# A decoder layer in float32r: new start addresses for the weight slots, and the transposed activations laid out four row tiles side by side

## The chip, the cores and the metric

The kernel runs on one core of a Trainium2 chip. The metric is the device time of one execution in microseconds (us). Before the change the median of three runs is 1054.98 us (1054.74 to 1055.16). A time that differs by less than 0.2% from another can't be told from it.

## The reference

One layer of a hybrid decoder over 1024 tokens of width 1024, batch 1, all in float32:

```python
h = rms_norm(x, mix_norm)
z = h @ w_in                        # one projection, columns cut among the two groups of heads
# group A: gated linear attention in chunks of 64, 4 heads, low-rank forget gate, SiLU output gate
# group B: sliding-window attention (128), 8 query and 2 key/value heads, ALiBi and sinks
x = x + concat([o_gla, o_swa]) @ w_out
h2 = rms_norm(x, ffn_norm)
u = causal_dwconv(h2 @ w_up, conv_w, conv_b)     # 3 taps over the tokens, 2 x 2816 columns
a, b = split(u, 2)
return x + (silu(a) * b) @ w_down
```

## The kernel before

**Precision by splitting.** Matmuls run on float32r operands. So that float32 accuracy is kept, each operand is held as two parts, hi (rounded) and lo (the rest), and each product is three matmuls: hi x hi, hi x lo, lo x hi (`PASSES`, L30). `split` (L90) makes the parts: ScalarE copies hi, then GpSimd or VectorE subtracts it from the source to give lo.

**Tiles that the change touches.** `big` (L65) holds the transposed activations, 64 KB a partition: for each of 8 row tiles `t` of 128 tokens and each of 8 blocks `k` of 128 channels, the hi and the lo block of 128 x 128. It is written once for the first norm (`tr_hi`, `tr_lo`), again with the heads' outputs (`gate_tr`), and again for the second norm (`norm_tr`, `norm2_sums`). `ex` (L657) holds three more operands of the same kind, made by `norm2_sums` for the up projection. The weights live in slots: nine tiles of 2 x 512 float32r (4096 bytes a partition) in the pool `wa` on the right side of the memory (`slot_tile`, L80), each holding hi and lo of one block; `w_tile` (L83) hands them out in the dense stage by the table `SLOTS`, with a tenth slot from another pool, used once (block 0 of the second half of `w_out`). `mhalf` is a tile of 32 bytes that holds the exponent -0.5 for GpSimd's `pow`.

**The dense stage.** `dense` (L313) makes 128 rows x 512 columns of a projection in one PSUM bank: 24 matmuls, the activations' block of `big` as the stationary operand (128 columns, one run), the weight slot as the moving one (512 columns, one run). `unit_q_part` (L700) does the same in pieces at the start. The projection to k, v of the window and the low-rank gate (`dk`) is 272 columns wide and takes seven of its eight weight blocks from a tile of its own, `kw`. Between these units stand the matmuls of the two attentions.

**The gated MLP.** The up projection goes through 22 chunks of 128 columns of each half. A chunk is a two-by-two block product done with seven block products in place of eight (a Strassen scheme): `up_operand` makes seven weight operands A11, A12, S4, A22, S1, S2, S3 in slots, `product` (L821) runs 12 matmuls for each with the weight slot as the stationary operand and four row tiles of `big` or `ex` as the moving one, 512 columns. These four row tiles are four runs of 128 elements, 8192 bytes apart in `big` and 4096 in `ex` (`b_operand`, L800). The operands A11 and A12 of chunk 1 lie outside the slots, in the pool `pn` (`U_SLOT` -1 and -2, L762). ScalarE and VectorE add the products, run the three taps and the gate. The down projection is made in the same way over pairs of chunks: `down_pair` (L1005) runs six matmuls into two PSUM banks, and one VectorE addition (L1019) puts both into `acc`; here both operands come from slots. `last_row` (L1032) does the last two chunks and writes the output.

**What sets the order.** Every step is entered with a due time into one list (`at`, L1053), and the list sorted by it is the program's order; the start is written out in `FIRST` (L1102). Units of the down projection stand between the up products, one after each product in the steady part. Neither depends on addresses.

**Where things lie.** In the built program `big` and `ex` begin at multiples of 64 bytes of each partition (1152 and 112448), so do `kw` (160320), the tenth slot (187840) and chunk 1's A11 and A12 (178240, 182336). The nine slots begin at 192480, 196576, ... 225248, each 32 past a multiple of 64, since `mhalf` (192448, 32 bytes) lies right below them and they fill the rest up to the end.

Of the kernel before, what the change touches and what calls it, by code (L numbers as in the profile page):

```python
# [9 lines left out]
F32 = mybir.dt.float32  # L10
F32R = mybir.dt.float32r
# [6 lines left out]
P = 128  # L18
T = 1024
D = 1024  # L20
NT = T // P
KD = D // P
# [12 lines left out]
def hymba_layer_kernel(ctx, tc, x, mix_norm, w_in, w_alpha2, b_alpha, gla_norm,  # L35
# [3 lines left out]
    act, dve, pool, pe, sp = nc.scalar, nc.vector, nc.gpsimd, nc.tensor, nc.sync  # L39
# [10 lines left out]
    base = ctx.enter_context(tc.tile_pool(name="base", bufs=1))  # L50
# [4 lines left out]
    def bank(name):  # L55
        ps["n"] += 1
        if "f" in ps:
            return ps["f"][2 + ps["n"] % 2]

        for start, which in (("n2pt_6", "b"), ("do1_7", "a"), ("n2pt_3", "a")):  # L60
            if name.startswith(start):
                return ps[which].tile([P, 512], F32, tag="b", name=name)
        return ps["ab"[ps["n"] % 2]].tile([P, 512], F32, tag="b", name=name)

    big = base.tile([P, NT, KD, 2, P], F32R, name="big")  # L65

    RAW_BUFS, K4, K2, N_WARM = 3, 6, 5, 5

    def raw_tile(name):
        return base.tile([P, 1024], F32, tag="raw", name=name, bufs=RAW_BUFS)  # L70

    w_keep = ctx.enter_context(tc.tile_pool(name="wa", bufs=1, side="right"))
    w_late = {}
    swp = ExitStack()
    idp = swp.enter_context(tc.tile_pool(name="idp", bufs=1, side="right"))
# [14 lines left out]
    def split(src, hi, lo, eng=None, hi_eng=None):  # L90
        if hi_eng is None:
            act.copy(hi, src)
        else:
            hi_eng.tensor_copy(hi, src)
        (eng or pool).tensor_sub(lo, src, hi.bitcast(F32))  # L95
# [19 lines left out]
    upper = gl.tile([P, P], F32, name="upper")  # L115
    amask = upper.bitcast(I32)
    ind = gl.tile([P, 2], F32R, name="ind")
    mhalf = idp.tile([P, 8], F32, name="mhalf")
    pool.memset(mhalf, -0.5)

    ones_r = gl.tile([P, P], F32R, name="ones_r")
# [64 lines left out]
    def norm1_tr(t, i):  # L186
        tr_hi(t, i, xts["h", t], "n1")

    def norm1_lo(t, i):
        tr_lo(t, i, "n1")  # L190
# [32 lines left out]
    def norm2_sums(t):  # L223

        i, ex, pn = t - 4, fin["ex"], fin["pn"]
        p0, p1 = fin["pb", t]

        def put(src, dst):
            split(src, dst[:, :, 0, :], dst[:, :, 1, :], dve)

        b12 = pn.tile([P, 4, P], F32, tag="b12", name=f"b12_{t}", bufs=1)
        b11, b21 = big[:, i, 0:4].bitcast(F32), big[:, i, 4:8].bitcast(F32)
        act.copy(b12, p0)
        put(p1, big[:, t, 4:8])
        dve.tensor_sub(p0, p0, b11[:, :, 0, :])
        dve.tensor_sub(p0, p0, b11[:, :, 1, :])
        put(p0, big[:, t, 0:4])
        dve.tensor_sub(p1, p1, b12)
        put(p1, ex[:, 1, i])
        dve.tensor_add(p1, p1, b11[:, :, 0, :])  # L240
        dve.tensor_add(p1, p1, b11[:, :, 1, :])
        put(p1, ex[:, 0, i])
        dve.tensor_sub(p0, b21[:, :, 0, :], p1)
        dve.tensor_add(p0, p0, b21[:, :, 1, :])
        put(p0, ex[:, 2, i])

    trs = {}

    def tr_hi(t, q, h, tag):
        pt = bank(f"{tag}pt_{t}_{q}")  # L250
        for k in range(4):
            c = (q * 4 + k) * P
            pe.transpose(pt[:, k * P:(k + 1) * P], h[:, c:c + P], ident)
        trs[tag, t, q] = pt.rearrange("p (k c) -> p k c", k=4)
        act.copy(big[:, t, q * 4:q * 4 + 4, 0, :], trs[tag, t, q])

    def tr_lo(t, q, tag):
        hi, lo = big[:, t, q * 4:q * 4 + 4, 0, :], big[:, t, q * 4:q * 4 + 4, 1, :]
        dve.tensor_sub(lo, trs[tag, t, q], hi.bitcast(F32))

    def norm_tr(t, h, tag):
# [5 lines left out]
    blocks = {}  # L267
# [45 lines left out]
    def dense(t, ws, n, name):  # L313
        pb = bank(name)
        for k in range(KD):
            for i, (ra, rb) in enumerate(PASSES):
                pe.matmul(pb[:, :n], lhsT=big[:, t, k, ra, :], rhs=ws[k][:, rb, :n],  # L317
                          start=(k == 0 and i == 0), stop=(k == KD - 1 and i == 2))
        return pb

# [299 lines left out]
    def gate_tr(t, gs):  # L620
        pb = bank(f"ogt{t}")
        for h in range(4):
            pe.transpose(pb[:, h * P:(h + 1) * P], gs[:, h * P:(h + 1) * P], ident)
        pv = pb.rearrange("p (h c) -> p h c", h=4)
        hi, lo = big[:, t, 0:4, 0, :], big[:, t, 0:4, 1, :]
        act.activation(hi, pv, AF.Copy, scale=glan)
        dve.scalar_tensor_tensor(lo, pv, glan, hi.bitcast(F32), op0=ALU.mult, op1=ALU.subtract)
        src = qo[:, t, :].rearrange("p (j c) -> p j c", j=4)
        hi, lo = big[:, t, 4:8, 0, :], big[:, t, 4:8, 1, :]
        split(src, hi, lo)  # L630


    fin = {}
# [19 lines left out]
    def open_norm2():  # L653
        st.close()
        w_late["pool"] = swp.enter_context(tc.tile_pool(name="wb", bufs=1, side="right"))
        xp = ctx.enter_context(tc.tile_pool(name="xp", bufs=1))
        fin["ex"] = xp.tile([P, 3, 4, 4, 2, P], F32R, name="ex")  # L657
        fin["sn"] = ExitStack()
        pn = fin["pn"] = fin["sn"].enter_context(tc.tile_pool(name="pn", bufs=1))
        ffn = fin["ffn"] = pn.tile([P, D], F32, name="ffn")  # L660
        sp.dma_start(ffn, ffn_norm.partition_broadcast(P).rearrange("p o d -> p (o d)"))
        fin["s1"] = pn.tile([P, 4, P], F32, name="s1_0")
# [37 lines left out]
    def unit_q_part(t, k0, k1):  # L700
        if k0 == 0:
            psb["q", t] = bank(f"dq{t}")
        pb = psb["q", t]
        for k in range(k0, k1):

            for i, (ra, rb) in enumerate(((0, 0), (1, 0), (0, 1))):
                pe.matmul(pb, lhsT=big[:, t, k, ra, :], rhs=blocks["q"][k][:, rb, :],  # L707
                          start=(k == 0 and i == 0), stop=(k == KD - 1 and i == 2))

    def q_done(t):  # L710
# [2 lines left out]
    def unit_q(t):  # L713
        q_post(t, dense(t, blocks["q"], 512, f"dq{t}"))

    def unit_k(t):
        kvl_post(t, dense(t, blocks["k"], 272, f"dk{t}"))

    def unit_v(t):
        act.activation(vg[0][:, t, :], dense(t, blocks["v"], 512, f"dv{t}"), AF.Copy, scale=row_scale(t))  # L720
# [78 lines left out]

    def b_operand(name, k, r):  # L800
        ex = fin["ex"]
        return {"B11": big[:, 0:4, k, r, :], "B21": big[:, 0:4, 4 + k, r, :],
                "B22": big[:, 4:8, 4 + k, r, :], "T1": big[:, 4:8, k, r, :],
                "T2": ex[:, 0, :, k, r, :], "T3": ex[:, 1, :, k, r, :],
                "T4": ex[:, 2, :, k, r, :]}[name]

    PROD = {"P1": ("A11", "B11"), "P2": ("A12", "B21"), "P3": ("S4", "B22"), "P4": ("A22", "T4"),
            "P5": ("S1", "T1"), "P6": ("S2", "T2"), "P7": ("S3", "T3")}
# [280 lines left out]
    for c in halves:  # L1089
        split(mix_row[:, c], mix_hl[0][0:1, c], mix_hl[1][0:1, c], dve)  # L1090
        pb = bank(f"mix{len(mix_ps)}")
# [4 lines left out]
    def mix_copy():  # L1096
        for c, pb in zip(halves, mix_ps):
# [3 lines left out]
    TU = TO + 16.0  # L1101
    FIRST = ((norm1_mul, 0, 0), (q_hi, 0), (q_lo, 0, pool), (norm1_mul, 0, 1), (warm_up, 2), (norm1_tr, 0, 0),  # L1102
             (norm1_lo, 0, 0), (q_hi, 1), (q_lo, 1, dve), (warm_up, 1), (norm1_tr, 0, 1), (warm_up, 2), (unit_q_part, 0, 0, 2), (q_hi, 2), (q_lo, 2, pool),
             (q_hi, 3), (norm1_mul, 1, 0), (q_lo, 3, dve), (unit_q_part, 0, 2, 3), (norm1_tr, 1, 0),
             (norm1_lo, 1, 0), (unit_q_part, 0, 3, 4), (q_hi, 4), (q_lo, 4, pool), (norm1_lo, 0, 1),
             (norm1_mul, 1, 1), (unit_q_part, 1, 0, 3), (q_hi, 5), (q_lo, 5, pool), (norm1_tr, 1, 1),
             (unit_q_part, 1, 3, 4), (norm1_lo, 1, 1), (q_hi, 6), (q_lo, 6, dve), (q_hi, 7), (q_lo, 7, pool),
# [25 lines left out]
    for t in range(NT):  # L1133
        if t > 1:
            if t > 3:
                at(t - 2.7, load_x, t)
                at(t - 2.5, norm1, t)
                at(t - 1.6, lambda tt=t: norm_tr(tt, xts["h", tt], "n1"))
            if t > 2:
                at(TQ + t, unit_q, t)  # L1140
        at(TK + 0.6 * t, unit_k, t)
        at(TK + 0.6 * t + 1.9, kvl_tr, t)
        at(TK + 0.6 * t + 3.1, kvl_la, t)
        at(TV + t, unit_v, t)
        at(TG + t, unit_g, t)
        at(TR + t, unit_r, t)
        at(TO + t, unit_o, t, 0)
        u = TO + 8 + (2 * t if t < 4 else 2 * t - 7)
        at(u, unit_o, t, 1)
        at(u + 0.005, norm2_rows, t)  # L1150
        if t < 7:
            at(u + 1.9, norm2_tr, t)
        if 4 <= t < 7:
            at(u + SUMS, norm2_sums, t)
# [56 lines left out]
    for ch, i, name in order:  # L1211
# [7 lines left out]
        if ch < 2 or (ch, i) == (2, 0):  # L1219
            n = 0  # L1220
        elif ch < L - 1 or (ch, i) == (L - 1, 0):
            n = 1
        else:
            n = 2
# [15 lines left out]
    at_us(-12, behind, first_sums)  # L1240
    at_us(0.28, norm2_tr, 7)
    at_us(0.29, norm2_sums, 7)
    at_us(1.76, load_side, 1, 1)
    for n, (ch, name, t0) in enumerate(prods):
# [4 lines left out]
    for p in range(NPAIR):  # L1249
        for k in range(7):  # L1250

            n = 7 * p + k - 2
# [51 lines left out]
```

## Time and profile before

| | |
|---|---|
| median of three runs | 1054.98 us |
| the profiled execution, first to last instruction (span) | 1053.6 us |
| TensorE busy | 1046.6 us, 4976 matmuls |
| VectorE busy | 799.4 us |
| GpSimd busy | 617.7 us |
| ScalarE busy | 480.2 us |
| granted TensorE clock, mean | 1.000 |

The page and the trace come from one execution. PE is TensorE's matmuls, PEld its weight loads, DVE VectorE, ACT ScalarE, POOL GpSimd, L317 line 317. Names are the program's with numbers left out: `fb<-big,A11w` is a matmul that reads `big` and the slot that holds A11, and writes a PSUM bank `fb`. Matmuls are pipelined, so the durations of neighbours overlap: how fast TensorE goes is read from the distance between starts. A row of the timeline gives the start of a group of like instructions, the time from its first start to its last end, and their number.

### The profile page before, as it was taken

The page shows a single profiled execution, that of the slowest core. Times are in us where ns is not written, and L with a number is a line of the kernel's source. Part 1 is how long each engine was busy: PE and PEld are TensorE (multiplying, and loading weights), DVE is VectorE, ACT ScalarE, POOL GpSimd, SP SyncE. Part 2 cuts the span into 40 slices and gives each one's busy share as a digit, 9 for nine tenths or more (in the row PEclk, how much of TensorE's full clock was granted, in tenths as well). Part 3 has the DMA queues.
Part 4 walks back from the last instruction along what each step waited for, and adds up shares of the span by engine and source line. Part 5 has one row for each costly group of instructions (what it writes and reads, how often), then busy time and mean ns, then how long its engine had stood idle before and what let it go on. Part 6 is the DMA issues. An engine that isn't in the chain of part 4 may idle for free.

```text
span 1053.6 us, 13921 instructions
## 1 busy us (share of the span) xinstructions
PE 1046.6 (99%) x4976; PEld 851.0 (81%) x4976; DVE 799.4 (76%) x1332; ACT 480.2 (46%) x988; POOL 617.7 (59%) x510
## 2 busy tenths in 40 slices
PE   9999999999999999999999999999999999999998
PEld 6898877888888888888888888888888888888887
DVE  6776667754131699887979898897979798897976
ACT  5527655444340346554444445444444444444441
POOL 4592132325450205867868687877778687978750
PEclk9999999999999999999999999999999999999999
DMA  6152113002044202112121111212121211121104
GB/s 213 61 152 61 44 49 92 21 1 81 1 122 159 60 1 80 40 41 81 40 80 34 49 51 49 60 61 61 40 80 40 61 40 45 56 61 60 41 20 160
DMA packets 67502, 67.13 MB, mean 64 GB/s; under 512 B 4648, under 2 KB 52201, under 8 KB 67434
## 3 DMA queue, kind: packets, MB, share of 16 engines
q1 hardware_dynamic: 63448, 61.27, 18.7%
q10 hardware_dynamic: 3986, 4.99, 2.0%
q8 instruction: 39, 0.64, 0.2%
q14 instruction: 29, 0.24, 0.1%
HBM read 57.33 MB, written 4.19 MB: 58 GB/s over the span
## 4 chain that ended last, share of the span: by engine, by line
PE 97%; DMA 1%; DVE 1%; ACT 0%; issue 0%; POOL 0%; DVEq 0%; ACTq 0%; SPq 0%
PE fb L834 39%; PE dn_P L1015 18%; PE do L317 9%; PE dr L317 4%; PE dv L317 4%; PE dg L317 4%; PE dq L317 3%; PE dk L317 2%; PE gb L834 2%; PE dq L707 1%; PE pv L490 1%; PE dl L1044 1%; PE fb L1044 1%; PE go L600 1%; PE ga L591 1%; PE sc L443 1%
## 5 line engine op out<-in xcount | busy, mean ns | idle before, releaser
L1019 DVE TENSOR_TENSOR acc<-acc,dn_P 128x1024 f32<-128x1024 f32 x140 | 169.8, 1214 | 65.6 <-PE dn_P L1015 65.5
L1015 PE MATMUL dn_P<-dw,dg 128*128 128x512 f32 x840 | 215.8, 392 | 0.0
L1015 PEld LDWEIGHTS dn_P<-dw,dg 128*128 128x128 f32 x840 | 157.7, 188 | 37.1
L317 PE MATMUL do<-wow,big 128*128 128x512 f32 x384 | 92.9, 398 | 0.0
L317 PEld LDWEIGHTS do<-wow,big 128*128 128x128 f32 x384 | 71.1, 188 | 16.3
L95 POOL TENSOR_TENSOR dw<-dn,dw 128x512 fp32r<-128x512 f32 x50 | 69.1, 1381 | 25.3 <-PE dn_P L1015 19.5
L886 ACT COPY ca<-fb 128x512 f32<-128x512 f32 x62 | 36.3, 585 | 72.8 <-PE fb L834 72.7
L834 PE MATMUL fb<-big,A11w 128*128 128x512 f32 x252 | 63.0, 396 | 0.0
L834 PE MATMUL fb<-big,S4w 128*128 128x512 f32 x252 | 62.9, 396 | 0.0
L834 PE MATMUL fb<-big,S1w 128*128 128x512 f32 x252 | 62.9, 396 | 0.0
L834 PE MATMUL fb<-ex,S2w 128*128 128x512 f32 x252 | 62.8, 396 | 0.0
L834 PE MATMUL fb<-ex,S3w 128*128 128x512 f32 x252 | 62.8, 396 | 0.0
L841 DVE SCALAR_TENSOR_TENSOR ua<-fb,cc,ua 128x511 f32<-128x511 f32 x84 | 62.2, 740 | 0.5 <-ACT ua L846 0.3
L834 PE MATMUL fb<-big,A12w 128*128 128x512 f32 x252 | 62.5, 396 | 0.0
L834 PE MATMUL fb<-ex,A22w 128*128 128x512 f32 x252 | 62.5, 397 | 0.0
L834 PEld LDWEIGHTS fb<-big,A11w 128*128 128x128 f32 x252 | 47.4, 188 | 11.6
L834 PEld LDWEIGHTS fb<-big,S1w 128*128 128x128 f32 x252 | 47.4, 188 | 11.6
L834 PEld LDWEIGHTS fb<-big,S4w 128*128 128x128 f32 x252 | 47.4, 188 | 11.6
L834 PEld LDWEIGHTS fb<-ex,S2w 128*128 128x128 f32 x252 | 47.4, 188 | 11.4
L834 PEld LDWEIGHTS fb<-ex,A22w 128*128 128x128 f32 x252 | 47.4, 188 | 11.4
L834 PEld LDWEIGHTS fb<-ex,S3w 128*128 128x128 f32 x252 | 47.4, 188 | 11.4
L834 PEld LDWEIGHTS fb<-big,A12w 128*128 128x128 f32 x252 | 47.3, 188 | 11.1
(432 smaller groups left out, 2402.7 us busy)
## 6 DMA issues: line engine op xcount, KB each, us to landing
up<-in_w_up_dram SPq DMA_DIRECT2D x44, 512.0 KB, 3.9
dn<-in_w_down_dram SPq DMA_DIRECT2D x22, 512.0 KB, 3.5
acc<-in_x_dram SPq DMA_DIRECT2D x8, 512.0 KB, 6.9
out_dram<-acc SPq DMA_DIRECT2D x15, 256.0 KB, 2.0
xt<-in_x_dram SPq DMA_DIRECT2D x7, 512.0 KB, 3.4
vraw<-in_w_in_dram SPq DMA_DIRECT2D x4, 512.0 KB, 3.7
graw<-in_w_in_dram SPq DMA_DIRECT2D x4, 512.0 KB, 3.6
qt<-qt ACTq DMA_DIRECT2D x16, 128.0 KB, 2.2
```

Source lines behind the costliest of these rows:

```text
L95: (eng or pool).tensor_sub(lo, src, hi.bitcast(F32))
L317: pe.matmul(pb[:, :n], lhsT=big[:, t, k, ra, :], rhs=ws[k][:, rb, :n], start=(k == 0 and i == 0), stop=(k == KD - 1 and i == 2))
L443: pe.matmul(pbs[-1][:, j % 2, :], lhsT=ql[:, g, qc], rhs=kt[:, g, kc], start=False, stop=True)
L490: pe.matmul(pbs[i][HALF[g]], lhsT=vv[rows, t - 1 + b, HALF[g]], rhs=rhs[rows, :, HALF[i]], start=start, stop=stop)
L591: pe.matmul(pb[:, pr * 256:(pr + 1) * 256], lhsT=gqt[t][:, pr, :], rhs=qbd[t % 2][:, pr], start=(pr == 0), stop=(pr == 1))
L600: pe.matmul(pb[:, h * P:(h + 1) * P], lhsT=asb[:, h, :], rhs=v[:, h * P:(h + 1) * P], start=(h == 0), stop=(t == 0 and h == 3))
L834: pe.matmul(pb, lhsT=w[:, ra, k, :], rhs=b_operand(bn, k, rb), start=(onto is None and i == 0), stop=(i == 11), skip_group_check=onto is n ...
L841: dve.scalar_tensor_tensor(dst, src, w, dst, op0=ALU.mult, op1=ALU.add)
L886: act.copy(dst, pb)
L1015: pe.matmul(pb[:, i], lhsT=g[:, ra, c:c + P], rhs=w[:, rb, :], start=(onto is None and n == 0), stop=(n == 2), skip_group_check=onto is no ...
L1019: dve.tensor_add(acc, acc, pb)
L1044: pe.matmul(pb[:, c0:c1], lhsT=g[:, ra, (t % 4) * P:(t % 4 + 1) * P], rhs=w[:, rb, c0:c1], start=(ch == NCH - 2 and i == 0), stop=(ch == N ...
```

## The change

`mhalf` moves into a pool of its own that is opened before the slots, and so lies above them at the top of the memory (229312 in the built program). The nine slots move down by 32 bytes, to 192448, 196544, ... 225216, all multiples of 64. No other tile moves.

`big` and `ex` keep their size and place but order their contents otherwise: for each half of the tokens, block `k` and part (hi or lo), the four row tiles of 128 tokens stand side by side. A new function `rows(t, ks, r)` gives one row tile's blocks. The moving operand of an up product is then one run of 512 elements; the stationary operand of the dense stage is one run of 128, as before. The writers of `big` and `ex` write four runs of 128 elements as before, at another distance (4096 bytes in place of 1024).

In the program as built, the instructions of all five engines stand in the same order as before, with the same shapes written and behind the same semaphores.

```diff
-    big = base.tile([P, NT, KD, 2, P], F32R, name="big")
+    big = base.tile([P, 2, KD, 2, 4, P], F32R, name="big")
+
+    def rows(t, ks, r):
+        return big[:, t // 4, ks, r, t % 4, :]
...
+    edge = ctx.enter_context(tc.tile_pool(name="edge", bufs=1, side="right"))
+    mhalf = edge.tile([P, 8], F32, name="mhalf")
     w_keep = ctx.enter_context(tc.tile_pool(name="wa", bufs=1, side="right"))
...
-    mhalf = idp.tile([P, 8], F32, name="mhalf")
     pool.memset(mhalf, -0.5)
...
-        put(p1, big[:, t, 4:8])
+        put(p1, *own(slice(4, 8)))
...
-        act.copy(big[:, t, q * 4:q * 4 + 4, 0, :], trs[tag, t, q])
+        act.copy(rows(t, slice(q * 4, q * 4 + 4), 0), trs[tag, t, q])
...
-                pe.matmul(pb[:, :n], lhsT=big[:, t, k, ra, :], rhs=ws[k][:, rb, :n],
+                pe.matmul(pb[:, :n], lhsT=rows(t, k, ra), rhs=ws[k][:, rb, :n],
...
-        fin["ex"] = xp.tile([P, 3, 4, 4, 2, P], F32R, name="ex")
+        fin["ex"] = xp.tile([P, 3, 4, 2, 4, P], F32R, name="ex")
...
-        return {"B11": big[:, 0:4, k, r, :], "B21": big[:, 0:4, 4 + k, r, :],
-                "B22": big[:, 4:8, 4 + k, r, :], "T1": big[:, 4:8, k, r, :],
-                "T2": ex[:, 0, :, k, r, :], "T3": ex[:, 1, :, k, r, :],
-                "T4": ex[:, 2, :, k, r, :]}[name]
+        return {"B11": big[:, 0, k, r], "B21": big[:, 0, 4 + k, r],
+                "B22": big[:, 1, 4 + k, r], "T1": big[:, 1, k, r],
+                "T2": ex[:, 0, k, r], "T3": ex[:, 1, k, r], "T4": ex[:, 2, k, r]}[name]
```

More of the change, by code (lines that the diff above doesn't have):

```diff
@@ L226, in norm2_sums, with put, extra, own @@
         p0, p1 = fin["pb", t]
-        def put(src, dst):
-            split(src, dst[:, :, 0, :], dst[:, :, 1, :], dve)
+        def put(src, hi, lo):
+            split(src, hi, lo, dve)
+        def extra(n):
+            return ex[:, n, :, 0, i, :], ex[:, n, :, 1, i, :]
+        def own(ks):
+            return rows(t, ks, 0), rows(t, ks, 1)
         b12 = pn.tile([P, 4, P], F32, tag="b12", name=f"b12_{t}", bufs=1)
-        b11, b21 = big[:, i, 0:4].bitcast(F32), big[:, i, 4:8].bitcast(F32)
+        b11, b21 = ([rows(i, ks, r).bitcast(F32) for r in range(2)] for ks in (slice(0, 4), slice(4, 8)))
         act.copy(b12, p0)
-        put(p1, big[:, t, 4:8])
-        dve.tensor_sub(p0, p0, b11[:, :, 0, :])
-        dve.tensor_sub(p0, p0, b11[:, :, 1, :])
-        put(p0, big[:, t, 0:4])
+        put(p1, *own(slice(4, 8)))
+        dve.tensor_sub(p0, p0, b11[0])
+        dve.tensor_sub(p0, p0, b11[1])
+        put(p0, *own(slice(0, 4)))
         dve.tensor_sub(p1, p1, b12)
[L239 to L245, printed above, removed]
+        put(p1, *extra(1))
+        dve.tensor_add(p1, p1, b11[0])
+        dve.tensor_add(p1, p1, b11[1])
+        put(p1, *extra(0))
+        dve.tensor_sub(p0, b21[0], p1)
+        dve.tensor_add(p0, p0, b21[1])
+        put(p0, *extra(2))
     trs = {}
@@ L254, in tr_hi @@
         trs[tag, t, q] = pt.rearrange("p (k c) -> p k c", k=4)
-        act.copy(big[:, t, q * 4:q * 4 + 4, 0, :], trs[tag, t, q])
+        act.copy(rows(t, slice(q * 4, q * 4 + 4), 0), trs[tag, t, q])
     def tr_lo(t, q, tag):
-        hi, lo = big[:, t, q * 4:q * 4 + 4, 0, :], big[:, t, q * 4:q * 4 + 4, 1, :]
+        hi, lo = (rows(t, slice(q * 4, q * 4 + 4), r) for r in range(2))
         dve.tensor_sub(lo, trs[tag, t, q], hi.bitcast(F32))
@@ L624, in gate_tr @@
         pv = pb.rearrange("p (h c) -> p h c", h=4)
-        hi, lo = big[:, t, 0:4, 0, :], big[:, t, 0:4, 1, :]
+        hi, lo = (rows(t, slice(0, 4), r) for r in range(2))
         act.activation(hi, pv, AF.Copy, scale=glan)
@@ L628, in gate_tr @@
         src = qo[:, t, :].rearrange("p (j c) -> p j c", j=4)
-        hi, lo = big[:, t, 4:8, 0, :], big[:, t, 4:8, 1, :]
+        hi, lo = (rows(t, slice(4, 8), r) for r in range(2))
         split(src, hi, lo)
@@ L706, in unit_q_part @@
             for i, (ra, rb) in enumerate(((0, 0), (1, 0), (0, 1))):
-                pe.matmul(pb, lhsT=big[:, t, k, ra, :], rhs=blocks["q"][k][:, rb, :],
+                pe.matmul(pb, lhsT=rows(t, k, ra), rhs=blocks["q"][k][:, rb, :],
                           start=(k == 0 and i == 0), stop=(k == KD - 1 and i == 2))
```

## The prediction

> **What bounds the kernel now.** I read the page first: busy shares and the chain that ended last.
>
> ```profile
> span 1053.6 us, 13921 instructions
> PE 1046.6 (99%) x4976; PEld 851.0 (81%) x4976; DVE 799.4 (76%) x1332; ACT 480.2 (46%) x988; POOL 617.7 (59%) x510
> PE 97%; DMA 1%; DVE 1%; ACT 0%; issue 0%; POOL 0%; DVEq 0%; ACTq 0%; SPq 0%
> ```
>
> TensorE is the chain. A busy TensorE could still be one that waits inside its work, so the second view is what TensorE waited for, all of it:
>
> ```profile
> PE warm L1085 <- DVE warm L124: 1.7, 1, 1.7
> PE dg L317 <- ACT vg L720: 0.9, 1, 0.9
> PE dq L707 <- POOL qw L295: 0.3, 1, 0.3
> PE gb L834 <- ACT big L255: 0.2, 1, 0.2
> PE dq L707 <- DVE big L259: 0.2, 1, 0.2
> ```
>
> That is 3.3 us in 1053.6. No other engine sets the end, so only the pace of the matmuls can move the time: how far apart two starts lie. The durations of the groups (near 396 ns) are no pace, since neighbours overlap. The pace comes from the timeline of TensorE: the next row's start less this row's, divided by the count. In the gated MLP:
>
> ```profile
> 559.86 1.54 PE L1015 MATMUL dn_P<-dw,dg 128*128 128x512 f32 x6
> 561.24 2.97 PE L834 MATMUL fb<-big,A12w 128*128 128x512 f32 x12
> 564.04 1.54 PE L1015 MATMUL dn_P<-dw,dg 128*128 128x512 f32 x6
> 565.42 2.98 PE L834 MATMUL fb<-ex,S2w 128*128 128x512 f32 x12
> 568.23 1.55 PE L1015 MATMUL dn_P<-dw,dg 128*128 128x512 f32 x6
> ```
>
> An up product takes 2.80 to 2.81 us for 12, some 234 ns each; a down unit 1.38 us for 6, some 230 ns. The dense stage, in one long row, and the last rows of the program:
>
> ```profile
> 317.70 18.60 PE L317 MATMUL do<-wow,big 128*128 128x512 f32 x79
> 1036.30 2.88 PE L1044 MATMUL fb<-dnw,g 128*128 128x512 f32 x12
> 1039.02 0.84 PE L1044 MATMUL dl<-dnw,g 128*128 128x512 f32 x3
> ```
>
> Dense: (18.60 - 0.39 for the last one's tail) / 78 = 233.5 ns. The last rows: 2.72 / 12 = 226.7 ns. So the same 128x512 matmul runs at 226.7 in one place, at 230 in another and at 233.5 to 234 in two more, with nothing waited for. That spread is what the change can act on.
>
> **The change, part by part.** It adds, removes and moves no instruction: on all five engines the same instructions stand in the same order, behind the same waits. Only addresses differ, in two ways.
>
> *Start addresses.* The nine weight slots began 32 bytes past a multiple of 64 and now begin on one. `big`, `ex` and the tenth slot did so already. In the four places above, stationary and moving operand were placed like this (offset past a multiple of 64): up products 32 and 0; dense 0 and 32; down units and last rows 32 and 32, since both come from slots. Where the two offsets are equal, the pace is 226.7 to 230; where they differ, 233.5 to 234. The kernel holds one more experiment: for chunk 1 the operands A11w and A12w lie in another pool, at offset 0. Same code, same `big`, some microseconds from the slots' A11w and A12w:
>
> ```profile
> 404.85 1.10 PE L834 MATMUL gb<-big,A11w 128*128 128x512 f32 x4
> 405.79 2.46 PE L834 MATMUL fb<-big,A11w 128*128 128x512 f32 x10
> 408.09 1.09 PE L834 MATMUL gb<-big,A12w 128*128 128x512 f32 x4
> 410.04 2.99 PE L834 MATMUL fb<-big,A12w 128*128 128x512 f32 x12
> 412.87 2.97 PE L834 MATMUL gb<-big,S4w 128*128 128x512 f32 x12
> ```
>
> The rows of gb (chunk 0, offset 32): 0.94 / 4 = 235 ns. Those of fb (chunk 1, offset 0): 2.30 / 10 = 230 ns, a change-over at each end included. This is the strongest line for the change: about 5 ns a matmul, with the moving operand still in four pieces.
>
> *One piece.* The moving operand of the up products was four runs of 512 bytes, 8192 bytes apart in `big`, 4096 in `ex`. Now it is one run of 2048. At unequal offsets the piece count costs little: dense reads one run at 233.5, the up products four at 233.3 to 234.2, so at most 0.7 ns. At equal offsets only the bounds are known: 226.7 (last rows, one run, both at 32) and 230 (chunk 1, four runs, both at 0). For one run with both at 0 there is the projection to k, whose seven slots of their own begin at 0; it is 272 columns wide:
>
> ```profile
> 61.79 13.47 PE L317 MATMUL dk<-kw,big 128*128 128x272 f32 x106
> ```
>
> (13.47 - 0.29) / 105 = 125.5 ns. From 272 to 512 columns at the last rows' pace is 226.7 - 125.5 = 101.2 ns for 240 columns, 0.42 ns a column: the two rows lie on one line, with 12 ns beside the columns in both. I take 226.7 for all 512-wide matmuls in one piece with both operands at 0, and keep 230 as the other end.
>
> The counts, by the groups of instructions:
>
> ```profile
> L834 PE MATMUL fb<-big,A11w 128*128 128x512 f32 x252 | 63.0, 396 | 0.0
> L1015 PE MATMUL dn_P<-dw,dg 128*128 128x512 f32 x840 | 215.8, 392 | 0.0
> L317 PE MATMUL do<-wow,big 128*128 128x512 f32 x384 | 92.9, 398 | 0.0
> L317 PE MATMUL dg<-gw,big 128*128 128x512 f32 x192 | 47.9, 403 | 0.9 <-ACT vg L720 0.9
> L317 PE MATMUL dr<-rw,big 128*128 128x512 f32 x192 | 47.5, 401 | 0.0
> L317 PE MATMUL dv<-vw,big 128*128 128x512 f32 x192 | 47.5, 400 | 0.0
> L317 PE MATMUL dq<-qw,big 128*128 128x512 f32 x120 | 29.3, 399 | 0.0
> L707 PE MATMUL dq<-qw,big 128*128 128x512 f32 x72 | 19.5, 408 | 0.6 <-POOL qw L295 0.3 <-DVE big L259 0.2
> ```
>
> Up: seven operands, 22 chunks of 12 (252 for chunks 1 to 21, 12 for chunk 0), 1848. Dense 512-wide: 384 + 3 x 192 + 120 + 72 = 1152. Down 840.
>
> - Up: 1824 x (234 - 226.7) + 24 x (230 - 226.7) = 13.4 us. Lower end, at 230: 7.3.
> - Dense: 1152 x (233.5 - 226.7) = 7.8 us; some 60 of these stand in the first 25 us, where weights arrive late, so 7.4. Lower end 0 (see the rivals).
> - Down: 840 x (230 - 226.7) = 2.8 us. Both operands move by the same 32 bytes, so nothing changes inside a unit; what goes is the change-over from products at unequal offsets. Lower end 0.
> - Last rows, k projection, transposes, the attention's own tiles: as before, 0.
>
> Sum 23.6 us. Against it stands what a faster TensorE meets. Its cover is thinnest in the MLP, where VectorE is the next engine:
>
> ```profile
> 560.00:650.00 90.00, 90.00 (x388) 72.60 (x387) 81.66 (x100) 42.28 (x72) 70.32 (x52) 1.00 0.16 47
> DVE acc L1019 <- PE dn_P L1015: 65.5, 61, 3.1
> ```
>
> (90 us: TensorE, weight loads, VectorE, ScalarE, GpSimd.) VectorE is busy 81.7 of 90. With TensorE 3% faster this work has 87.3 us, 94%. It still fits, and at 61 of its 140 additions into `acc` VectorE today waits for TensorE (65.5 us). But in the other 79 it comes late, and a bank that it frees late can now stop TensorE, for at most a 1.2 us addition. I take off 2 us (bounds 0 and 6). VectorE's own instructions don't change with the slots' start:
>
> ```profile
> 351.85 0.69 DVE L95 TENSOR_TENSOR A11w<-up,A11w 128x512 fp32r<-128x512 f32 x1 [0.56 <-ACT A11w L92]
> 359.45 0.69 DVE L95 TENSOR_TENSOR A11w<-up,A11w 128x512 fp32r<-128x512 f32 x1
> ```
>
> The first writes a slot at offset 32, the second chunk 1's tile at 0: both 0.69 us. The writes into `big` and `ex` keep runs of 512 bytes, so I cost them at nothing. Moving the 32-byte tile of exponents costs nothing: the same instructions read it.
>
> Net 23.6 - 2 = 21.6 us. The profiled span of 1053.6 lies 1.4 us under the median of the runs (1054.98), so 1054.98 - 21.6 = 1033.4 us.
>
> A rule that speaks against this: the Trainium skill, "SBUF — State Buffer", Specifications (TRN2), gives lines of 16 bytes and asks for two hits on each for full bandwidth. By it a start 32 bytes off and runs of 512 bytes cost nothing, and the sum would be 0 in place of 23.6 (the third rival). Chunk 1's 230 against 235 ns disagrees.
>
> **The rivals.**
>
> *Half the gain.* The pace settles at chunk 1's 230 rather than at 226.7, or the dense stage gains nothing. For the latter speak the only dense matmuls whose slot is already at 0, the first three of each row tile of the second half of `do`:
>
> ```profile
> 349.20 1.10 PE L317 MATMUL do<-wow,big 128*128 128x512 f32 x4
> 392.79 1.09 PE L317 MATMUL do<-wow,big 128*128 128x512 f32 x4
> ```
>
> These are one matmul before and the first three: (1.10 - 0.39) / 3 = 237 and 233 ns, no better than the rest. Against it: they come straight out of a shifted stretch, and the first down matmuls behind a product are slow as well (230 for six, where twelve in a row give 226.7). All at 230: up 7.3, dense 3.8, down 0, last rows -0.3, less 1 for waits: 9.8, so 1045. Without dense but at 226.7: 16.2 - 1.5 = 14.7, so 1040. Middle 1042.5.
>
> *VectorE takes over in the MLP.* If its waits there don't shrink, that stretch keeps its length and only the dense 7.4 us are won: 1047.6. Against: 6% of its time stays free.
>
> *The start doesn't matter.* Chunk 1 was quick for another reason, and only the one piece counts: 1848 x 0.7 = 1.3 us, so 1053.7, no change.
>
> *Slower.* One run with both operands at 0 is itself the bad case, as the 237 ns of the first row above would have it: then every matmul of the three kinds goes there. Up +3 x 1848 = 5.5, dense +3.5 x 1152 = 4.0, down +7 x 840 = 5.9, together +15.4: 1070. It decides as soon as the up products' pace is above 234. Against: the k projection with both at 0 lies on the fast line.
>
> *Much faster.* 226.7 isn't the floor, and with both at 0 what lies beside the columns shrinks from 12 ns to a few. At 3 ns: 9 ns more for 3840 matmuls, 34.6 us, so 999. Against: chunk 1 and k, already at 0, show no sign of it. The Trainium skill ("TensorE: Matmul & The Clock Gate", Back-to-back issue gap) states 2.5 ns beside the columns; no row here shows it for these matmuls.
>
> **How the numbers follow.** Forecast 1033.4: chance 0.52. Half the gain 0.29, VectorE 0.06, no change 0.06, slower 0.04, much faster 0.03. The forecast's own range is 1029.5 (no waits, 1031.4, and another 0.5 ns on 3840 matmuls, which rows read to 0.01 us can't show) to 1037.4 (6 us of waits); 8 in 10 needs most of half the gain as well, up to 1044. Below 0.2%, 2.1 us, a change can't be told from none here. Faster: 0.52 + 0.29 + 0.06 + 0.03 = 0.90. Same 0.06, slower 0.04.
>
> **What would show it.** In the changed kernel's timeline a product of 12 should take 2.72 us instead of 2.81, a down unit 1.36 instead of 1.38, 79 dense matmuls 18.1 instead of 18.6. TensorE's waits should stay under 6 us. A product at 2.75 means half the gain; at 2.81 the offsets don't matter; above it, the slower rival. A product at 2.72 with a span over 1040 puts the loss on waits, to be looked for at VectorE's addition L1019.

## The result

The changed kernel takes 1048.1 us (median, 1046.85 to 1048.91) against 1054.86 before; the ratio is 0.9936, 95% interval 0.9922 to 0.995. It is faster, by 0.6%, where 2.0% was forecast: 6.8 us instead of 21.6, and outside the range that was stated (to 1044). The page of the changed kernel:

```profile
span 1047.2 us, 13921 instructions
PE 1039.3 (99%) x4976; PEld 849.6 (81%) x4976; DVE 799.0 (76%) x1332; ACT 480.3 (46%) x988; POOL 618.5 (59%) x510
```

TensorE is the bound as before. All that it waited for (engine, line, what for, us in total, times, longest):

```profile
PE warm L1094 <- DVE warm L128: 1.7, 1, 1.7
PE sc L453 <- DMA ql<-ql: 1.0, 1, 1.0
PE dg L327 <- ACT vg L730: 0.9, 1, 0.9
PE dq L717 <- POOL qw L305: 0.3, 1, 0.3
PE gb L843 <- ACT big L265: 0.2, 1, 0.2
PE dq L717 <- DVE big L269: 0.2, 1, 0.2
```

So 4.3 us in place of 3.3: the missing 15 us did not go into waits. They are missing in the pace. TensorE's timeline in the gated MLP and in the dense stage, in the same stretches as before (start, time to the last end, group, count):

```profile
561.09 2.95 PE L843 MATMUL fb<-ex,S2w 128*128 128x512 f32 x12
563.88 1.54 PE L1024 MATMUL dn_P<-dw,dg 128*128 128x512 f32 x6
565.25 2.96 PE L843 MATMUL fb<-big,S1w 128*128 128x512 f32 x12
568.05 1.54 PE L1024 MATMUL dn_P<-dw,dg 128*128 128x512 f32 x6
...
312.76 23.51 PE L327 MATMUL do<-wow,big 128*128 128x512 f32 x102
```

An up product takes 2.79 us on `ex` and 2.80 on `big`, not the 2.72 that the forecast needs: 233 ns a matmul. A down unit is at 1.37 to 1.38 us. The dense stage has gained: (23.51 - 0.39) / 101 = 228.9 ns instead of 233.5. The means of all distances between starts in each kind, without gaps over 260 ns, account for the result:

| matmuls of 512 columns | before, ns | after, ns | count | us |
|---|---|---|---|---|
| dense | 233.3 | 229.4 | 1092 | -4.3 |
| up, on `big` | 234.0 | 233.2 | 1056 | -0.8 |
| up, on `ex` | 234.5 | 232.6 | 792 | -1.5 |
| down | 230.4 | 229.7 | 840 | -0.5 |

That is -7.1 us (dense without the 60 of the first 25 us), and TensorE waits 1.0 us more; the spans differ by 6.4, the runs by 6.8.

Chunk 1, on which the argument rested, tells something too. In the changed kernel its A11w runs next to slots that begin at a multiple of 64 like itself:

```profile
402.07 2.50 PE L843 MATMUL fb<-big,A11w 128*128 128x512 f32 x10
404.40 1.08 PE L843 MATMUL gb<-big,A12w 128*128 128x512 f32 x4
405.33 0.39 PE L843 MATMUL fb<-big,A11w 128*128 128x512 f32 x1
405.56 1.03 PE L224 MATMUL fb<-ident,n2h 128*128 128x128 f32 x8
406.35 3.00 PE L843 MATMUL fb<-big,A12w 128*128 128x512 f32 x12
409.18 2.96 PE L843 MATMUL gb<-big,S4w 128*128 128x512 f32 x12
```

Its A11w takes 2.33 / 10 = 233 ns, where it took 230 before. Its A12w takes 2.83 us for 12 with 0.31 us of that behind the transposes, so 2.52 / 11 = 229. Same offsets, same layout, two paces: the offset within 64 bytes can't be the whole cause.

### The profile page after: what moved, and what is told of

Same layout as the page of the kernel before. It is cut to its first block, busy times and chain, and to the rows that moved or that the text cites. A ratio compares the mean times of both kernels' runs of the same rounds, so it can differ in the third digit from the quotient of the medians.

```text
span 1047.2 us, 13921 instructions
## 1 busy us (share of the span) xinstructions
PE 1039.3 (99%) x4976; PEld 849.6 (81%) x4976; DVE 799.0 (76%) x1332; ACT 480.3 (46%) x988; POOL 618.5 (59%) x510
## 4 chain that ended last, share of the span: by engine, by line
PE 97%; DMA 1%; DVE 1%; ACT 0%; issue 0%; POOL 0%; DVEq 0%; ACTq 0%; SPq 0%
PE fb L843 39%; PE dn_P L1024 18%; PE do L327 8%; PE dr L327 4%; PE dv L327 4%; PE dg L327 4%; PE dq L327 3%; PE dk L327 2%; PE gb L843 2%; PE dq L717 1%; PE pv L500 1%; PE dl L1053 1%; PE fb L1053 1%; PE go L610 1%; PE ga L601 1%; PE sc L453 1%
```

## The experiments

Three theories went in. **A**: the new start gives the up products 5 ns, and the one piece takes them away. **B**: the start helps only where the slot is the moving operand. **C**: what counts is the distance between the two operands' addresses modulo some power of two above 64; down units and last rows, both operands from slots 4096 bytes apart, would have distance 0 and for that reason the best pace. **D**, beside them: with the same addresses several rhythms (sequences of distances between starts that repeat) are possible, and what ran ahead decides.

### The two halves of the change apart

The start alone, the layout left as before:

```diff
+    edge = ctx.enter_context(tc.tile_pool(name="edge", bufs=1, side="right"))
+    mhalf = edge.tile([P, 8], F32, name="mhalf")
     w_keep = ctx.enter_context(tc.tile_pool(name="wa", bufs=1, side="right"))
...
-    mhalf = idp.tile([P, 8], F32, name="mhalf")
```

> The slots begin at multiples of 64 as in the change, the activations keep their four runs. Theory A (the one piece takes away in the up products what the new start gives them there, because chunk 1's A11w, in four runs with both operands at 0, ran at 230 ns before and at 233 in the changed kernel): up products at 229 to 230 ns instead of 234.2, dense at 229 as in the changed kernel, down as before; 1824 x 5 = 9 us and 1100 x 4.2 = 4.6 us, so 1041 us, ratio 0.987, faster than the change. Theory B (the start matters only where the slot is the moving operand, and chunk 1 was quick for a reason of its own): up stays at 234, only dense gains, 1050 us, ratio 0.9955.

Measured: 1048.11 us, ratio 0.9936 (0.9921 to 0.995), the change's own time. TensorE's timeline:

```profile
560.09 2.96 PE L835 MATMUL fb<-ex,S2w 128*128 128x512 f32 x12
562.88 1.54 PE L1016 MATMUL dn_P<-dw,dg 128*128 128x512 f32 x6
564.26 2.96 PE L835 MATMUL fb<-big,S1w 128*128 128x512 f32 x12
567.06 1.54 PE L1016 MATMUL dn_P<-dw,dg 128*128 128x512 f32 x6
```

2.79 and 2.80 us a product, with four runs, as with one. Theory A, which had 1041 us, falls: the piece count takes nothing away. B had 1050 us, with the up products left at 234 ns (they are at 233), and misses narrowly.

The layout alone, `mhalf` left in its old place:

```diff
-    edge = ctx.enter_context(tc.tile_pool(name="edge", bufs=1, side="right"))
-    mhalf = edge.tile([P, 8], F32, name="mhalf")
...
+    mhalf = idp.tile([P, 8], F32, name="mhalf")
     pool.memset(mhalf, -0.5)
```

> The activations lie in one run, the slots begin 32 past a multiple of 64 as before. Theory A: with unequal offsets the number of runs matters little, up at 233.3, dense unchanged at 233.4; 1 to 2 us, ratio 0.9985 to 1. Theory B says the one piece is what took the up products from 234.2 to 233.2 in the changed kernel: the same 1 to 2 us here. If it is slower than before, the one piece costs time by itself.

Measured: 1055.02 us, ratio 1.0003 (0.9993 to 1.0012). One run instead of four is worth nothing that can be told from 0, where A and B allowed 1 to 2 us: all of the gain comes from moving the slots by 32 bytes.

```profile
561.03 2.97 PE L842 MATMUL fb<-big,A12w 128*128 128x512 f32 x12
563.83 1.54 PE L1023 MATMUL dn_P<-dw,dg 128*128 128x512 f32 x6
565.21 2.98 PE L842 MATMUL fb<-ex,S2w 128*128 128x512 f32 x12
568.02 1.55 PE L1023 MATMUL dn_P<-dw,dg 128*128 128x512 f32 x6
```

2.80 and 2.81 us a product: the rows from before the change.

### The slots another 64 bytes lower

This tells C from A and B. The starts stay at multiples of 64; the distance to `big` becomes 0 modulo 256.

```diff
-    mhalf = edge.tile([P, 8], F32, name="mhalf")
+    mhalf = edge.tile([P, 24], F32, name="mhalf")
```

> The changed kernel with its slots another 64 bytes lower, so still at multiples of 64. Theory A and B, which know only the offset within 64 bytes: the same paces and time as the changed kernel, 1048 us, ratio 0.9936. Theory C (what counts is the distance between the two operands' addresses modulo some larger power of two; before, down units have distance 0 modulo 512 and the fastest pace): the distance of the slots from the tile big becomes 0 modulo 256 instead of 64, and up products on big and the dense stage go to 227 ns: another 1000 x 6 + 1100 x 2 = 8 us, ratio 0.986.

Measured: 1039.13 us, ratio 0.985 (0.9836 to 0.9865), another 9 us. TensorE's timeline:

```profile
561.15 2.88 PE L843 MATMUL fb<-big,S1w 128*128 128x512 f32 x12
563.87 1.52 PE L1024 MATMUL dn_P<-dw,dg 128*128 128x512 f32 x6
565.23 2.96 PE L843 MATMUL fb<-ex,S3w 128*128 128x512 f32 x12
568.03 1.54 PE L1024 MATMUL dn_P<-dw,dg 128*128 128x512 f32 x6
...
314.65 15.58 PE L327 MATMUL do<-wow,big 128*128 128x512 f32 x68
```

Products on `big`: 2.72 us, 226.7 ns. Products on `ex`, whose distance to the slots went from 128 to 192, stay at 2.80. Down units behind a `big` product take 1.36 us, behind an `ex` product 1.38 (the first is 565.23 - 563.87). Dense: (15.58 - 0.39) / 67 = 226.7 ns. Neither A nor B has room for this. C holds. The pools that were opened after the slots on that side of the memory move with them, but the four kinds of matmul alone account for some 8.9 us of the 9.7 between the two spans, and the wait of 1.0 us that this kernel does not have covers the rest.

### The pace against the distance, measured by itself

A kernel of bare matmuls, 128x512, in groups of 30 behind four transposes, the starts of the operands moved from group to group (one execution; the granted clock was 1.00 through all groups):

```diff
+    for n, (kind, order, s, a) in enumerate(CONFIGS):
+        separate()                      # four transposes
...
+                if kind == "up":        # weight slot stationary; activations in one run
+                    lhs = slots[:, s + ra * 512 + k * P:][:, :P]
+                    rhs = acts[:, a + (k * 2 + rb) * 512:][:, :512]
...
+                elif kind == "dense":   # activations stationary, a slot for each block k moving
+                    lhs = acts[:, a + (k * 2 + ra) * 512:][:, :P]
+                    rhs = slots[:, s + k * 1024 + rb * 512:][:, :512]
```

> No layer is computed: 63 groups of 30 matmuls of 128x512, each group behind four transposes, with the operands laid out as in the up products (slot stationary, activations moving in one run or four), the dense stage (activations stationary, slot moving) and the down units (both from slots), at starts that differ by 0 to 512 bytes, in the order of the passes that the kernel uses and in the reverse one. Only the pace within each group is read. Theory A: pace falls into two classes by the offsets within 64 bytes, equal 227 to 229, unequal 233, four runs quicker than one at equal offsets. Theory C: pace depends on the distance over a longer range than 64 bytes, with a minimum of 227 at distance 0. Theory D (several rhythms are possible with the same addresses, and what runs ahead decides): groups with the same offsets modulo 64 all show the same pace here, since all are entered alike, 229 for the one run too.

Four of the groups in TensorE's timeline: slots moved by 32, 192, 224 and 256 bytes.

```profile
27.14 7.24 PE L141 MATMUL bank<-acts,slots 128*128 128x512 f32 x30
...
64.34 7.14 PE L141 MATMUL bank<-acts,slots 128*128 128x512 f32 x30
...
71.66 7.24 PE L141 MATMUL bank<-acts,slots 128*128 128x512 f32 x30
...
79.09 7.09 PE L141 MATMUL bank<-acts,slots 128*128 128x512 f32 x30
```

7.24 against 7.09 us is 0.15 over some 28 matmuls, 5 ns each. The means of the last 24 distances between starts, by the distance "start of the moving operand less start of the stationary one", modulo 256 (ns):

| distance | up, one run | up, four runs | dense | up, passes reversed |
|---|---|---|---|---|
| 0 | 226.7 to 228.0 | 227.1 to 227.8 | 226.6, 227.0 | 226.8 |
| 32 | 233.3, 233.4 | | 233.3 | |
| 64 | 228.9, 229.0 | 228.9 | 228.9 | 228.9 |
| 96 | 233.3 to 233.8 | | 233.8 | |
| 128 | 232.1 to 232.7 | 232.7 | 232.6 | 232.7 |
| 160 | 234.4, 234.5 | 234.4 | | |
| 192 | 233.3, 233.4 | 233.3 | 233.3 | 233.3 |
| 224 | 233.3 | 233.2, 233.4 | | 233.3 |

(At distance 0 each group ends at 226.7; means above that still hold some of the first matmuls.) Behind the transposes the pace is a function of this distance. Which operand is moved, whether it lies in one run or four, which of the two is the slot, and the order of the three passes make no difference. With the addresses of the kernels it gives these paces:

| distance (pace by the table, ns) | dense | up on `big` | up on `ex` | chunk 1 | down |
|---|---|---|---|---|---|
| before; one piece alone | 96 (233.3) | 160 (234.4) | 96 (233.3) | 64 (228.9) | 0 (226.7) |
| changed; start alone | 64 (228.9) | 192 (233.3) | 128 (232.7) | 64 (228.9) | 0 |
| slots 64 lower | 0 (226.7) | 0 (226.7) | 192 (233.3) | 64 | 0 |

The traces have the dense and up paces within 0.5 ns, with two exceptions. The products on `ex` ran at 234.5 before, where the bare matmuls at distance 96 give 233.3 to 233.8; that nanosecond stays open. And the first matmuls behind something else (the change-over) are slower, so that all of the dense stage together, at distance 0, comes to 228.2 ns and only its long rows to 226.7. The down units, six matmuls each, are above the table for the same reason until the products beside them have distance 0 too.

### All distances 0

If so, the tile `ex` needs only 64 bytes more. Two small tiles of the convolution's edges went above the slots to make room; with `mhalf` they fill the 96 bytes that the run with the slots 64 lower used there.

```diff
     mhalf = edge.tile([P, 8], F32, name="mhalf")
+    edges = [edge.tile([P, 8], F32, name=f"edge{i}") for i in range(2)]
...
+        xp.tile([P, 16], F32, name="pad")
         fin["ex"] = xp.tile([P, 3, 4, 2, 4, P], F32R, name="ex")
...
-        e = psb[key, ch] = fin["ff"].tile([P, 2], F32, tag="e", name=f"{key}_{ch}", bufs=2)
+        e = psb[key, ch] = edges[(ch + (key == "e2")) % 2][:, 0:2]
```

> As the run with the slots 64 lower, and the tile ex 64 bytes higher (two small tiles of the convolution's edges go above the slots to make room), so that slots, big, ex and chunk 1's A11w and A12w all have distance 0 modulo 256. Theory C: the up products on ex, still at 233.3 ns there, go to 227 as those on big did; 792 + some first-chunk matmuls x 6.4 = 5.1 us, and the down units behind them lose their change-over, 840 x 1 = 0.8; 1039.1 - 5.9 = 1033 us, ratio 0.979 to 0.980. Theory A or B: no change against the run with the slots 64 lower, 1039.

Measured: 1033.25 us, ratio 0.9794 (0.9781 to 0.9808): the best of all, 22 us faster than before and 15 faster than the change.

```profile
562.52 1.52 PE L1026 MATMUL dn_P<-dw,dg 128*128 128x512 f32 x6
563.88 2.88 PE L845 MATMUL fb<-ex,S3w 128*128 128x512 f32 x12
566.60 1.52 PE L1026 MATMUL dn_P<-dw,dg 128*128 128x512 f32 x6
567.96 2.88 PE L845 MATMUL fb<-big,S4w 128*128 128x512 f32 x12
...
560.00:650.00 90.00, 90.00 (x398) 74.54 (x397) 79.49 (x100) 43.37 (x76) 67.22 (x50) 1.00 0.20 59
DVE acc L1030 <- PE dn_P L1026: 55.2, 50, 2.9
...
PE warm L1096 <- DVE warm L129: 1.7, 1, 1.7
PE dg L328 <- ACT vg L732: 1.0, 1, 1.0
PE dq L719 <- POOL qw L306: 0.3, 1, 0.3
PE gb L845 <- ACT big L266: 0.2, 1, 0.2
PE dq L719 <- DVE big L270: 0.2, 1, 0.2
```

Here every product takes 2.72 us and every down unit 1.36. The rows behind them are the stretch from 560 to 650 us (TensorE, weight loads, VectorE, ScalarE, GpSimd), VectorE's wait for the down matmuls over the whole execution, and all that TensorE waited for. VectorE waits 55.2 us for TensorE where it waited 65.5 before, so it has given up 10 us of its slack, and no product is later for it: TensorE's own waits are 3.4 us, against 3.3 before.

The same addresses with the old layout, four runs (the diff is the start's and the one above, without the change's layout):

> The same addresses, but big and ex keep the layout from before, four runs of 512 bytes for each moving operand. Theory C: the number of runs plays no part, 1033 us as with one run, within 1 us of it. If one run helps at distance 0, this is slower: at 1 ns a matmul by 1.8 us.

Measured: 1033.72 us, ratio 0.9798 (0.9784 to 0.9811). One run and four can't be told apart here either.

### Widths, finer starts, and what runs ahead

The bare matmuls once more, with starts that differ by 4 to 56 bytes, with fewer columns, and with groups that follow each other without transposes:

```diff
+        if sep:
+            separate()
...
+                pe.matmul(bank[:, :w], lhsT=lhs, rhs=rhs[:, :w], start=(i == 0 and j == 0), stop=(i == NSTEP - 1 and j == 2))
```

> No layer is computed: 53 groups of 30 matmuls, only their pace is read. Starts that differ by 4 to 56 bytes; 128 to 512 moving columns at distances 0, 64, 96, 128, 160 and 192; distances that follow each other with no transposes between; and distances that differ by multiples of 256. Theory C: 256 more or less changes nothing; the extra over the columns' own time at 512 columns is some 13 ns at distance 0 and 20 at 96 to 192, and if it comes from the weight load, which is as long whatever the columns, it is the same at 256 and 384 columns; if it comes from the moving operand's reading it shrinks with the columns. Theory D: a group entered straight from another distance keeps that one's rhythm; without it, it settles on its own pace within some 6 matmuls.

Adding 256, 512 or 1280 to one start changes nothing beyond 1 ns (226.8 to 227.7 at distance 0), nor does 768 at distance 64 (228.9). Between multiples of 32: the slots 16 bytes on, 226.7; 8 on, 230.7; 4 on, 232.3; 24 on, 231.1; 40, 48 and 56 on, 233.3. By the number of columns, the mean of the last 24 distances between starts (ns):

| columns | distance 0 | 64 | 96 | 128 | 160 | 192 |
|---|---|---|---|---|---|---|
| 128 | 111.7 | 111.7 | 111.7 | 111.7 | 111.7 | 111.7 |
| 256 | 120.0 | 117.8 | 120.0 | 118.8 | 118.6 | 113.3 |
| 272 | 125.2 | 126.7 | 125.5 | 126.7 | 123.4 | 123.3 |
| 384 | 173.8 | 173.3 | 176.7 | 175.6 | 173.3 | 176.7 |
| 512 | 227.1 | 228.9 | 233.3 | 232.7 | 234.4 | 233.3 |

The best distance is another one for another width: 192 at 256 columns, 0 at 512. So "distance 0" is no general rule, and neither of my two guesses on the extra (the same at all widths, or shrinking with the columns) holds.

Five groups without transposes, at distances 192, 64, 192, 0 and 64, stand in one row:

```profile
222.06 34.93 PE L132 MATMUL bank<-acts,slots 128*128 128x512 f32 x150
```

Their paces are 233.3, 233.3, 233.3, 226.8 and 228.9 ns. The second, at distance 64, kept the rhythm of the group ahead of it (233, 233, 234 ns, again and again) to its end. The last, at the same distance but entered from distance 0, ran at 229, 226, 232. In the same kernel a group at 64 behind one at 128 ran at 233.3, and one behind 224 at 228.9. So D is right for distance 64: two rhythms, and what ran ahead decides. It explains why chunk 1's A11w, entered from slots at distance 192, stayed at 233 in the changed kernel, in the same rhythm (233, 233, 234), and its A12w, behind transposes, ran at 229. Before the change the same A11w, entered from distance 160, had settled on 226, 229, 232. At distance 0 every group came to 226.7, behind transposes and, in the one case here, behind distance 192.

## Why the prediction was wrong

**What bounds the kernel** was right, and is what made the experiments quick to read: TensorE's pace between starts, and not its waits (3.2 to 4.3 us), moved the time in every run of the layer.

**Start addresses: the step that failed.** I sorted the paces by the offset of each operand past a multiple of 64 and concluded that equal offsets give 226.7 to 230 and unequal ones 233.5. What counts is the distance between the operands modulo 256. Equal offsets leave four distances, 0, 64, 128 and 192, which run at 226.7, 228.9, 232.7 and 233.3. The fast places before had distance 0 (down units and last rows, both from slots 4096 bytes apart) and 64 (chunk 1). The change made the offsets equal and the distances 64 in the dense stage, 192 for the products on `big`, 128 for those on `ex`. So the dense stage gained 4 ns of the 6.8 that I had put down for it, and the up products 0.8 and 1.9 of 7.3. The strongest line, chunk 1's 230 against 235 ns, was a true difference of distance, 64 against 160; the change gives that distance to the dense stage, but not to the up products, where the slot is the other operand of the two.

**One piece**: I bounded its worth by 0.7 ns at unequal offsets, left 3.3 ns open at equal ones, and took all of it. It is worth nothing that can be measured in all three pairs of kernels (1.0003 alone; 1048.11 against 1048.1 with the start; 1033.72 against 1033.25 at distance 0).

**The k projection as the row for "both at 0"** misled in three ways. A part of `kw` is 272 columns, 1088 bytes, so its blocks and parts don't have one distance but 192, 64, 0 and 128 in turn. At 272 columns these run at 123.3, 126.7, 125.2 and 126.7 ns (the second kernel of bare matmuls), in another order than at 512; weighted by their use, with the eighth block at distance 96, an estimate from these figures is 125.2, and the row had 125.5. And two rows always lie on one line: that it passes through the last rows supported nothing.

**The rows that spoke against it**, the first three dense matmuls with the tenth slot at 233 and 237 ns, were set aside as a change-over. Whether they were one, or the slower of the two rhythms at distance 64, three matmuls can't tell; at this distance the dense stage of the changed kernel runs at 229. Change-overs and steady paces had to be told apart in the up products too, where ten matmuls of chunk 1, at distance 64, stood for 1824.

**Down units**: right in mechanism. Inside a unit nothing changes; the change-over behind a product would go if the products had the units' distance. It did not go in the changed kernel (229.7 ns) and did with all distances 0 (226.7).

**The size of the sum**: with every distance at 0 the kernel takes 1033.25 us, where 1033.4 was forecast. It is not the case that the change makes, and that the two meet so closely is partly luck. The up products gain 13.7 us there and the down units 3.1, where 13.4 and 2.8 were forecast. The dense stage gains 5.6 and not 7.4, since its matmuls come to 228.2 ns together. The 2 us for waits of a faster TensorE were not needed: with all distances 0 VectorE still waits for it 55.2 us, and TensorE's own waits are 3.4 us.

**The rivals**: in number "VectorE takes over" came nearest (1047.6), and it too had the dense stage gain and the MLP not (they gained 4.3 and 2.8 us). That is luck, since its cause did not come: none of TensorE's 4.3 us of waits in the changed kernel is for an addition of the MLP, and with all distances 0 the products run at 226.7 beside the same VectorE. "Half the gain" had the dense stage right (229) in one variant, but the up products at 230; its other variant had the up products gain and the dense stage not, the reverse of what came. "The start doesn't matter", "slower" and "much faster" did not come: no steady pace at 512 columns was under 226.7. None of the rivals went by the distance.

## What to carry to other kernels

Where TensorE is the bound and waits for nothing, read its pace from the starts, kind by kind, and compare kinds that differ in their addresses: here 32 bytes in the place of a tile were worth 0.6%, another 64 bytes 0.9%, and 64 bytes for one more tile 0.6%, with not one instruction changed. Alignment to 64 bytes was the wrong question here; sort the paces by the distance between the start of the moving and of the stationary operand, modulo 256 in this case and for the width at hand, and measure that table by itself, which takes one short kernel. And where a handful of matmuls stands for thousands, ask in which other ways they differ.

## What the runs showed of the hardware

- The pace of matmuls depends on the relative address of their two operands: 226.7 to 234.5 ns for 128x512 in float32r with a new weight load each time, and the same again 256 bytes on. Why, and which part of the memory or of TensorE has this period, the runs don't show.
- From distance 0, a shift of 16 bytes costs nothing (226.7), one of 4 or 8 bytes 5.6 or 4.0 ns, one of 32 or 48 bytes 6.6. The Trainium skill ("SBUF — State Buffer", Specifications (TRN2)) speaks of lines of 16 bytes; the free shift by 16 agrees, the cost of 32 has no place in that rule.
- At 128 columns the pace is 111.7 ns at all six distances measured, so there something else sets it; from 256 columns on the distance counts, by up to 6.7 ns at 256 (113.3 to 120.0) and 7.7 at 512 (226.7 to 234.4).
- At distance 64 two steady rhythms exist, 229 and 233 ns. Behind distances 192 and 128 a group took the slower, behind 0, 224 and transposes the faster, and it kept it to the end of its 30 matmuls.
- Reading 2048 bytes in one run or in four runs, 4096 or 8192 bytes apart, makes no difference to TensorE's pace: 228.9 to 229.0 ns either way at distance 64, 232.1 to 232.7 at 128.
